# A decoder block in FP32: the first FFN chunk with three interleaved Strassen units and norm weights applied behind the transposes

## The chip, the core and the metric

The kernel runs on one core of one Trainium2 chip. The metric is the device time of one execution in microseconds, and of a set of executions the median. TensorE is written PE, ScalarE ACT, VectorE DVE, GpSimd POOL and SyncE SP.

## What is computed

One layer over 512 tokens of width 1024, all in float32: a retention branch and a block-sparse attention branch, mixed by sigmoid gates, an output product with a residual, and then the SwiGLU FFN with a hidden width of 2816. The change touches the end of the first part and the start of the FFN:

```python
mix = jax.nn.sigmoid(ga) * a + jax.nn.sigmoid(gb) * b
x = x + mix @ w_o[l]
h2 = rmsnorm(x, norm2_w[l])
f = (jax.nn.silu(h2 @ w_ffn_gate[l]) * (h2 @ w_ffn_up[l])) @ w_ffn_down[l]
x = x + f
```

with `rmsnorm(x, w) = x * rsqrt(mean(x*x) + 1e-6) * w`.

## The kernel before

**Number format.** Every operand of a large product is split into a high part in the reduced format fp32r (a cast on ACT, tiles `wh` for weights and `h`, first half, for activations) and a low part, the remainder (a subtraction on DVE, tiles `wl` and `h`, second half). `mm3` issues three matmuls for one product: high x high, high x low, low x high.

**Strassen units.** Most of the large products are done in the Strassen-Winograd form: seven products of quarter matrices instead of eight. The activations are the quarters A11, A12 (upper 256 tokens, first and second half of the features), A21, A22 (lower 256 tokens) and the sums S1 = A21 + A22 up to sign, S2, S3, S4, made by DVE and split like all else. The weights are B11, B21, B22 and the sums T1, T2, T3, T4: T1 and T3 come by a load and an accumulating transfer on POOL's queue, T2 is a sum on DVE, T4 is a sum on DVE or an accumulating transfer into T2's buffer once T2 has been split (`was_split`, L380). A unit (`wino_unit`) covers 128 gate columns twice and 128 up columns twice, two tiles of the hidden width. Each product is 2 x 4 calls of `mm3`, 24 matmuls. Its results are collected in PSUM banks X, Y and Z; Z is one bank for the whole program (`zbank`, in the trace `pm_233`). X is copied out behind B11 (`p1`, into `fa`) and behind T2 (`u2`, into `fb`), because T2 and T3 go on accumulating in it; Y behind T1 (`p5`). Z takes A12 x B21, which `c11` adds to the copy of X.

**The FFN.** `CHUNKS = (6, 6, 6, 4)` tiles of the hidden width, in units of two. The first chunk has three units: the first (`PLAIN`, `plain_unit`) is done without Strassen as eight products, four with the upper tokens and then four with the lower; the second has the order `DOWN`, the third `ENDING`. After each chunk comes its share of the down product. `Hidden` holds what happens to the results of a unit: Silu of the gate half, product with the up half, and the split and sums for the down product.

**Between the two parts.** The output product `w_o` is a unit with `Residual(squares, 0.5)`: its results are added to `xr`, squared on ACT with a sum (`squares`), and when a half of the tokens is complete `norm_rows` makes the row factor and `xn = xr * factor * norm weights` on DVE. `turned` transposes `xn` on PE, four transposes for two feature tiles; `h2_put` splits straight out of PSUM; `keep` in `h2_turn` also copies the whole into `f`, which the sums need. For the upper tokens this happens during the last product of `w_o`, at the places that `TURN` gives. For the lower tokens `h2_lower` does it after the third product of the plain unit (`before_last`), all 16 transposes in a row, and then plans the sums S1 to S4 with `later(n, ...)`, n half-products further.

**Order of the work.** Nothing is scheduled by the tool: each engine does its instructions in the order in which the program writes them. `advance`, called after each half product, counts the ticks of `later` and emits the split of the next weight piece (`piece_emit`) as far as the caps (`PAHEAD`, `FAHEAD`) allow; `porder` is the order of the pieces, `loads` that of the loads. A load is issued on SP when a raw buffer comes free (`used`).

Of the kernel before, what the change touches and what calls it, by code (L numbers as in the profile page):

```python
# [51 lines left out]
WARM = 12  # L52
T4CHUNKS = 52
LANE = 4
TURN = (0, 1, 2, 1)
WQ = 2
RGATE = (2, 0)
SUMS = 2
# [2 lines left out]
OAHEAD = (6, 10)  # L61
SLACK = 1000
MARGIN = 0
HLAG = 1
LLAG = 1
CHUNKS = (6, 6, 6, 4)
# [5 lines left out]
V_N1, V_Q, V_K = 0, 8, 9  # L72
V_ALL = 10

NORMAL = "B11 T1 *1 T2 B21 B22 T3 / T4"
ENDING = "B11 T1 *1 T2 B21 B22 T3 T4w"
PLAIN = "B11 B21 B12 B22"  # L80
DOWN = "B11 B21 T1 T2 B22 T3 / T4"
ALONE = "B11 B21 T1 T2 B22 T3 T4z"


def weight_plan():

    units = []

# [12 lines left out]

    halves = (range(4), range(4, 8))  # L110

    def cols(col):
        units.append(("X", ("w_in", halves, col, 256), NORMAL))

    units += [("M", (C_MQ, 0)), ("M", (C_MQ, 4)), ("M", (C_MK, 0)), ("M", (C_MK, 4))]
    cols(C_MV)
    for name, i in ORDER:
        if name == "rg":
            cols(C_RG + 512 * i)
        elif name == "rv":  # L120
            cols(C_RV + 512 * i)
        elif name == "rk":
            wino("w_in", C_RQ + 256 * i, "w_in", C_RK + 256 * i)
        elif name == "a":
            feat(sum([group("w_ret_out", (4 * i + ct) * P, KT) for ct in range(4)], []))
        elif name == "b":
            feat(sum([group("w_moba_out", (4 * i + ct) * P, 4) for ct in range(4)], []))
        else:
            c = {"ga": C_GA, "gb": C_GB}[name] + 512 * i
            wino("w_in", c + 256, "w_in", c)  # L130
    units.append(("X", ("w_o", halves, 0, 512), ALONE))
    for c in range(len(CHUNKS)):
# [32 lines left out]


@with_exitstack
def hybrid_block(ctx: ExitStack, tc: tile.TileContext, wall, xin, xtok, n2, cin, out):
    nc = tc.nc
    plan = weight_plan()  # L170
    NU = len(plan)
# [89 lines left out]
    def later(n, f):  # L261
        later_q.append([n, f])
# [21 lines left out]
    for u, unit in enumerate(plan):  # L284
        chunk_of[u] = chunk
        if unit[0] in "WX":
# [7 lines left out]
            if unit[2] == PLAIN:  # L294
                loads += [(u, (q, 0), [chunk + c]) for q, c in (("B11", 0), ("B21", 3), ("B12", 1), ("B22", 2))]
                porder += [(u, (q, 0)) for q in order]
                for q in order:
                    width[u, (q, 0)] = 1024
# [30 lines left out]
    def load_w(parts=1, queue=None):  # L329
        if wstate["load"] >= len(loads):  # L330
            return []
        u, q, cs = loads[wstate["load"]]
        wstate["load"] += 1
        t = raw[u, q] = big(nm("raw"))
        uses[u, q] = 2 if isinstance(q, tuple) and plan[u][2] != PLAIN and (q[0] == "B22" or q[0] == "B21" and u not in t4dma) else 1
# [438 lines left out]
    def wino_finish():  # L774
        if wpend:
            wpend.pop(0)()

    def wino_prod(w, u, bank, m, q, start, stop, out, copies=None, hold=False):

        kind, what = plan[u][:2]  # L780
# [2 lines left out]
        for j, n in enumerate(ws):  # L783
            pc = piece(u, (q, j))
            for i in (0, 1):
# [16 lines left out]
                advance(0 if hold and (j, i) != (0, 0) or copies and (j, i) in ((len(ws) - 2, 1), (len(ws) - 1, 0)) else 1)  # L802
# [6 lines left out]
    def wino_unit(w, ev, hooks={}):  # L809

        u = cur[0]
        cur[0] += 1
# [9 lines left out]

        def third(*x):
            ev.c22(*x)
            if "T4w" in order:
                ev.u3(*x)

        def first(*x):
            ev.p1(*([*x, bank("Z")] if seed else x))

        whole = "T4w" in order or "T4z" in order
# [8 lines left out]
        def run(q):  # L840
# [2 lines left out]
                      bank("Z") if q == "T3" and "T4z" in order else None,  # L843
                      q == "T4z")

        rest = False
        for q in order:
            if q == "/":
# [6 lines left out]
            else:  # L855
                run(q)
                if q in hooks:
                    hooks[q]()

    def plain_unit(w, ev, before_last):  # L860

        u = cur[0]
        cur[0] += 1
        for r in (0, 1):
            for n, out in enumerate((ev.gate, ev.up)):
                ps = main_ps()
                for x, q in enumerate((("B11", "B21"), ("B12", "B22"))[n]):
                    if (r, n, x) == (0, 1, 1):
                        before_last()
                    pc = piece(u, (q, 0))  # L870
                    for i in (0, 1):
                        for k in range(4):
                            mm3(ps[:, i * 256:(i + 1) * 256], pc[:, (4 * i + k) * P:(4 * i + k + 1) * P],
                                w(("A11", "A12", "A21", "A22")[2 * r + x], k), i == k == x == 0, x == 1 and k == 3, True)
                        if (r, i) == (1, 1):
                            piece_done(u, (q, 0))
                        advance(1)
                        run_bg(1)
                later(1, lambda r=r, ps=ps, out=out: out(r, ps))

    class Quarters:

# [554 lines left out]
    n2r = big("n2r")  # L1437
    nc.sync.dma_start(n2r, n2)

    class Residual:  # L1440

# [60 lines left out]
    h2 = Wino("h2")  # L1502

# [16 lines left out]

    def h2_turn(r):

        pss = []

        def keep(j):
            if j % 2 == 0:
                f2[r, j], f2[r, j + 1] = halves(nm("f"))
            A.copy(f2[r, j], pss[j])  # L1528

        def step(j):  # L1530
            pss.append(turned(r, j))
            h2_put(("A11", "A12", "A21", "A22")[2 * r + j // 2], j % 2, pss[j])()
            if j:
                keep(j - 1)
            if j == 3:
                keep(3)
                del xn[2 * r], xn[2 * r + 1]

        return [lambda j=j: step(j) for j in range(4)]
# [1 line left out]
    def h2_lower():  # L1541
# [13 lines left out]
        def rest():  # L1555
            lows.pop(0)()
            lows.pop(0)()

        later(1, lambda: sums_of("S1", (1, 2), (1, 0)))
# [4 lines left out]
        later(6, lambda: sums_of("S3", (0, 0), (1, 0)))  # L1564
        later(6, rest)
        later(7, rest)

    wstate["cap"] = OAHEAD
    more_raws(OEXTRA)
# [12 lines left out]
    assert not turn  # L1582


    class Hidden:
# [43 lines left out]
        def gate(self, r, x):  # L1629
            A.activation((self.a0, self.a1)[r], x, AF.Silu)  # L1630

        def up(self, r, x):
            if r:
                self.lower(x)
            else:
                self.upper(x)

        def upper(self, up):

# [53 lines left out]
    for c in range(len(CHUNKS)):  # L1693
# [7 lines left out]
                later_step()  # L1701
            return mats[m, k]

        for k, f in enumerate(chunk_tiles(c)[::2]):
            if f == 0:
                wstate["cap"] = PAHEAD
                plain_unit(h2, Hidden(mats, k), h2_lower)
            else:
                wstate["cap"] = FAHEAD
# [68 lines left out]
```

## Time and profile before

| | us |
|---|---|
| runs, lowest / median / highest of 3 | 782.83 / 783.02 / 783.41 |
| the profiled execution | 781.12 |
| its span | 779.2 |
| PE busy in it | 772.2 |
| DVE busy | 630.3 |
| ACT busy | 457.2 |

The span runs from the first to the last instruction of the profiled execution; its own time has what lies around that as well. Instructions of an engine overlap a little at their ends, so the time from one start to the next is shorter than a row's duration. Nearly all of the code is issued through one helper, so its line L220 says nothing; the operations are told apart by the names of their tiles.

### The profile page before, as it was taken

To read this page: it belongs to the slowest core of one execution; us is meant where nothing else is said; L and a number is where in the kernel's file an instruction comes from. 1 tells how busy PE (TensorE), PEld (TensorE's weight loads), DVE (VectorE), ACT (ScalarE), POOL (GpSimd) and SP (SyncE) were. 2 spreads that over 40 slices of the span, in tenths; PEclk is the share of its full clock that TensorE was granted. 3 is DMA by queue.
4 is the path that set the end of the run, shared out by engine and by line. 5 is a ranking of instruction groups with operands and counts; after the bars stand their busy time and mean duration, and the time that the engine had idled before them with its cause. 6 is when DMAs were issued, how large, how long until landed. Compare 5 with 4: busy or idle time off the path is not lost.

```text
span 779.2 us, 13656 instructions
## 1 busy us (share of the span) xinstructions
PE 772.2 (99%) x5394; PEld 711.6 (91%) x5394; DVE 630.3 (81%) x959; ACT 457.2 (59%) x750; POOL 69.0 (9%) x83
## 2 busy tenths in 40 slices
PE   9999999999999999999999999999999999999997
PEld 6889988899999998989988898988999899988996
DVE  7988778897788687758589798899787987789787
ACT  8655677774695485634356765654554455655442
POOL 0000100010101000000001000111001110110000
PEclk9999999999999999999999999999999999999999
DMA  9854753556677484654999614789556894779502
GB/s 325 284 130 114 162 131 88 136 140 159 188 167 187 124 221 114 166 133 127 256 328 257 167 32 108 180 208 298 163 137 161 258 269 109 170 200 287 128 1 108
DMA packets 40671, 134.86 MB, mean 173 GB/s; under 512 B 4512, under 2 KB 5024, under 8 KB 40608
## 3 DMA queue, kind: packets, MB, share of 16 engines
q1 hardware_dynamic: 28512, 93.75, 34.5%
q0 software_dynamic: 11376, 39.06, 28.7%
q10 hardware_dynamic: 720, 1.18, 0.4%
q8 instruction: 42, 0.69, 0.4%
q14 instruction: 21, 0.17, 0.1%
HBM read 131.88 MB, written 2.10 MB: 172 GB/s over the span
## 4 chain that ended last, share of the span: by engine, by line
PE 87%; DVE 6%; issue 3%; DMA 2%; ACT 1%; POOL 0%; DVEq 0%; ACTq 0%; POOLq 0%
PE pm L220 79%; PE ps L220 8%; DMA raw<-wall 2%; DVE wl L220 1%; DVE h L220 1%; DVE ws L220 1%; DVE xn L220 1%; DVE xr L220 0%; ACT wh L416 0%; ACT f L1528 0%; DVE mx L220 0%; POOL raw L343 0%; ACT h L1516 0%; ACT sq L1485 0%; DVE qb L220 0%
## 5 line engine op out<-in xcount | busy, mean ns | idle before, releaser
L220 DVE TENSOR_TENSOR wl<-raw,wh 128x1024 fp32r<-128x1024 f32 x209 | 252.2, 1220 | 39.5 <-ACT wh L416 32.7
L416 ACT CAST wh<-raw 128x1024 fp32r<-128x1024 f32 (+1 forms) x230 | 225.1, 1008 | 50.5 <-DVE raw L220 28.7
L220 PE MATMUL pm<-h,wh 128*128 128x256 f32 x1248 | 225.4, 283 | 1.6 <-ACT fa L1595 0.8
L220 PEld LDWEIGHTS pm<-h,wh 128*128 128x128 f32 x1248 | 195.0, 192 | 2.5 <-ACT fa L1595 1.0
L220 PE MATMUL pm<-h,wl 128*128 128x256 f32 x624 | 176.6, 283 | 0.0
L220 PEld LDWEIGHTS pm<-h,wl 128*128 128x128 f32 x624 | 119.7, 192 | 0.0
L343 POOL DMA_DIRECT2D raw<-wall x60 | 55.4, 924 | 442.1 <-DMA raw<-wall 244.0
L220 PE MATMUL pm<-hS,wh 128*128 128x256 f32 x384 | 71.0, 285 | 0.0
L220 PE MATMUL pm<-wh,hA 128*128 128x256 f32 (+1 forms) x304 | 68.6, 310 | 0.0
L220 PE MATMUL pm<-wh,hS 128*128 128x256 f32 x320 | 62.5, 286 | 0.0
L220 PEld LDWEIGHTS pm<-hS,wh 128*128 128x128 f32 x384 | 60.0, 192 | 0.6 <-issue 0.3
L220 PE MATMUL pm<-hS,wl 128*128 128x256 f32 x192 | 54.3, 283 | 0.0
L220 PE MATMUL pm<-hA,wh 128*128 128x256 f32 x288 | 53.7, 285 | 0.0
L220 PEld LDWEIGHTS pm<-wh,hA 128*128 128x128 f32 x304 | 50.9, 191 | 2.8 <-ACT p L1060 0.2
L220 PEld LDWEIGHTS pm<-wh,hS 128*128 128x128 f32 x320 | 51.5, 191 | 0.0
L220 DVE TENSOR_TENSOR raw<-raw,raw 128x1024 f32<-128x1024 f32 (+1 forms) x41 | 48.2, 1181 | 0.4
L220 PE MATMUL pm<-wl,hA 128*128 128x256 f32 (+1 forms) x152 | 46.4, 305 | 0.0
L220 PEld LDWEIGHTS pm<-hA,wh 128*128 128x128 f32 x288 | 45.2, 192 | 0.4
L220 PE MATMUL pm<-wl,hS 128*128 128x256 f32 x160 | 45.2, 283 | 0.0
L220 PE MATMUL pm<-hA,wl 128*128 128x256 f32 x144 | 40.7, 283 | 0.0
L220 PE MATMUL pm<-wh,gsh 128*128 128x512 f32 x112 | 39.8, 390 | 0.0
L220 PE MATMUL pm<-ret,wh 128*128 128x512 f32 x128 | 39.5, 390 | 0.0
(250 smaller groups left out, 1393.4 us busy)
## 6 DMA issues: line engine op xcount, KB each, us to landing
raw<-wall SPq DMA_DIRECT2D x155, 512.0 KB, 4.8
raw<-wall POOLq DMA_DIRECT2D x70, 512.0 KB, 7.0
raw<-wall SPq DMA_DIRECT2D x19, 256.0 KB, 3.5
raw<-wall POOLq DMA_DIRECT2D x9, 256.0 KB, 7.3
xr<-xtok SPq DMA_DIRECT2D x4, 512.0 KB, 7.2
x<-xin SPq DMA_DIRECT2D x7, 256.0 KB, 5.0
out<-xr SPq DMA_DIRECT2D x7, 256.0 KB, 2.1
raw<-wall ACTq DMA_DIRECT2D x4, 256.0 KB, 6.2
```

The lines of the kernel that those rows point to most:

```text
L220: return f(out, *args, **kw)
L343: nc.gpsimd.dma_start(t[:, s], wall[c, :, s], accum_op=ALU.add)
L416: A.copy(h, src)
```

## The change

1. All three units of the first chunk become Strassen units (`FIRST`), and their products are interleaved by a table, `SCRIPT`. The number ahead of a product is that of the unit. The six products B11 and B21 of the three units come first; they need upper tokens only. Then unit 0's T1, T2, B22, T3, and the rest. `plain_unit` goes; `wino_unit` is cut in two, and `wino_start` gives a function that runs one product.
2. T4 of all three comes by an accumulating transfer (`t4dma`). The last one has a bank of its own (T4w).
3. `h2_lower` is called after the third product as before, which now is unit 1's B11 (`LOWER`).
4. The norm weights are no longer in `xn`. The upper `xn` is a `tensor_scalar` on DVE, the lower one an ACTIVATE with a scale on ACT. Behind the transposes the features lie on the partitions, and two ACTIVATEs of 256 columns with the norm weight as scale (`vec[:, V_N2 + ...]`) make `f` out of PSUM; `h2_put` splits from `f`. A21 is not split any more, since no Strassen product reads it; A22 is split at the end (`last`). The transfer of the norm weights in row form (`n2r`) goes.
5. `TURN` has five places for the upper transposes instead of four: two of the four sets now stand in the middle of unit 0's first product.
6. In that first product one tick of `advance` emits no weight piece.

```diff
-TURN = (0, 1, 2, 1)
+TURN = (0, 1, 1, 0, 2)
+LOWER = "1 B11"
-PLAIN = "B11 B21 B12 B22"
+FIRST = "B11 B21 T1 T2 B22 T3 T4"
+SCRIPT = ("0 B11", "0 B21", "1 B11", "1 B21", "2 B11", "2 B21", "0 T1", "0 T2", "0 B22", "0 T3", "1 T1", "0 T4",
+          "1 T2", "1 B22", "1 T3", "2 T1", "1 T4", "2 T2", "2 B22", "2 T3", "2 T4w")
...
-            order = ENDING if f == fs[-2] else NORMAL
-            if f < 4:
-                order = (PLAIN, DOWN)[f // 2]
+            order = FIRST if c == 0 else ENDING if f == fs[-2] else NORMAL
...
+            if unit[2] == FIRST:
+                t4dma.add(u)
+                if plan[u - 1][2] != FIRST:
+                    table = dict(WLOAD)
+                    for x in SCRIPT:
+                        v, q = int(x[0]), x[2:5].rstrip("w")
+                        porder.append((u + v, (q, 0)))
+                        if q in table:
+                            loads.append((u + v, (q, 0), [chunk + 4 * v + c for c in table[q]]))
...
-                V.scalar_tensor_tensor(xn[2 * r + i][:, c], xr[2 * r + i][:, c], y[:, i:i + 1], n2r[:, c],
-                                       ALU.mult, ALU.mult)
+                o, x, f = xn[2 * r + i][:, c], xr[2 * r + i][:, c], y[:, i:i + 1]
+                if r:
+                    A.activation(o, x, AF.Copy, scale=f)
+                else:
+                    V.tensor_scalar(o, x, f, None, ALU.mult)
...
-            A.copy(f2[r, j], pss[j])
-
-        def step(j):
-            pss.append(turned(r, j))
-            h2_put(("A11", "A12", "A21", "A22")[2 * r + j // 2], j % 2, pss[j])()
+            f = f2[r, j]
+            for k in (0, 1):
+                c = slice(k * 256, (k + 1) * 256)
+                A.activation(f[:, c], ps[:, c], AF.Copy, scale=vec[:, V_N2 + 2 * j + k:V_N2 + 2 * j + k + 1])
+            if r == 0:
+                h2_put(("A11", "A12")[j // 2], j % 2, f)()
...
+        if c == 0:
+            wstate["cap"] = PAHEAD
+            runs = [wino_start(h2, Hidden(mats, k))[0] for k in range(CHUNKS[0] // 2)]
+            for x in SCRIPT:
+                runs[int(x[0])](x[2:])
+                if x == LOWER:
+                    h2_lower()
+                if x == "0 T1":
+                    wstate["cap"] = FAHEAD
```

Three places show how the engines' queues change. The first is ACT at the transposes of the upper tokens, behind the weight casts. Tiles `ps` are the transposed sets, `h` the split quarters A11 and A12, `sq` the squares of the lower tokens. Before:

```order
L1516 CAST h_638_5109<-ps_5104 128x512
L1485 ACTIVATE sq_5118,ss_4780<-xr_4772 128x512
L1516 CAST h_641_5125<-ps_5120 128x512
L1528 COPY f_5128<-ps_5104 128x512
L1516 CAST h_644_5135<-ps_5130 128x512
L1528 COPY f_5128<-ps_5120 128x512
```

Now:

```order
L1528 ACTIVATE f_5108<-ps_5103,vec 128x256 x2
L1512 CAST h_639_5111<-f_5108 128x512
L1478 ACTIVATE sq_5120,ss_4778<-xr_4772 128x512
L1528 ACTIVATE f_5108<-ps_5122,vec 128x256 x2
L1512 CAST h_642_5129<-f_5108 128x512
```

The cast of the first set no longer reads PSUM; it follows two scalings (the row with x2) and reads their result, and the second set follows a square as before.

The second is ACT from the row factor of the lower tokens (`r_s`) to their transposes; `wh` are weight casts, `ps` the transposed sets of the lower tokens. Before:

```order
L509 ACTIVATE r_s<-n2v 128x2
L416 CAST wh_5213<-raw_4914 128x1024
L1630 ACT_TABLE_LOAD
L1630 ACTIVATE fa_5159<-pm_5161 128x512
L1516 CAST h_662_5272<-ps_5267 128x512
L1516 CAST h_664_5280<-ps_5275 128x512
L1528 COPY f_5283<-ps_5267 128x512
L1516 CAST h_667_5290<-ps_5285 128x512
```

Now:

```order
L1494 ACTIVATE xn_5210<-xr_4772,r_y 128x512
L1494 ACTIVATE xn_5211<-xr_4773,r_y 128x512
L1596 COPY fa_5141<-pm_5147 128x512
L423 CAST wh_5229<-raw_4888 128x1024
L423 CAST wh_5245<-raw_4912 128x1024
L1608 ACT_TABLE_LOAD
L1608 ACTIVATE fa_5141<-fa_5141 128x512
L423 CAST wh_5264<-raw_4932 128x1024
L1528 ACTIVATE f_5286<-ps_5281,vec 128x256 x2
L1528 ACTIVATE f_5286<-ps_5289,vec 128x256 x2
L1528 ACTIVATE f_5301<-ps_5296,vec 128x256 x2
L1528 ACTIVATE f_5301<-ps_5304,vec 128x256 x2
```

The four `xn` have come to this queue from DVE, a third weight cast and the `fa` of unit 0's gate half stand ahead of the transposes' readers, and each reader is a pair of scalings.

The third is DVE from the first sum of S1 to the add out of the Z bank (`fa` from `pm_233`). Before, that add stood behind the whole of the plain unit; the rows from S1's sums on are:

```order
L220 TENSOR_TENSOR ws_5317<-f_5302,f_5283 128x512
L220 TENSOR_TENSOR ws_5321<-f_5302,f_5283 128x512
L220 SCALAR_TENSOR_TENSOR ws_5337<-ws_5317,f_5128 128x512
L220 SCALAR_TENSOR_TENSOR ws_5341<-ws_5321,f_5128 128x512
L220 TENSOR_TENSOR h_672_5319<-ws_5317,h_672_5319 128x512
L220 TENSOR_TENSOR h_674_5323<-ws_5321,h_674_5323 128x512
L220 TENSOR_TENSOR fb_5160<-pm_5241,fa_5159 128x512
L220 TENSOR_TENSOR h_676_5339<-ws_5337,h_676_5339 128x512
```

Now:

```order
L223 TENSOR_TENSOR ws_5324<-f_5301,f_5286 128x512
L223 TENSOR_TENSOR ws_5328<-f_5301,f_5286 128x512
L223 SCALAR_TENSOR_TENSOR ws_5348<-ws_5324,f_5108 128x512
L223 SCALAR_TENSOR_TENSOR ws_5352<-ws_5328,f_5108 128x512
L223 TENSOR_TENSOR h_674_5326<-ws_5324,h_674_5326 128x512
L223 TENSOR_TENSOR h_676_5330<-ws_5328,h_676_5330 128x512
L223 TENSOR_TENSOR wl_5358<-raw_4932,wh_5332 128x1024
L223 TENSOR_TENSOR wl_5361<-raw_4953,wh_5334 128x1024
L223 TENSOR_TENSOR fa_5143<-pm_233,fa_5143 128x512
```

The last row is the add of unit 1. The sums S1 and S2, S1's low parts and the low parts of two weight pieces stand directly ahead of it.

## Rows read from the trace of the kernel before

**Rows 1.** The page, part 1: the span, and TensorE's busy time, share and matmuls.

```profile
span 779.2 us, 13656 instructions
...
PE 772.2 (99%) x5394; PEld 711.6 (91%) x5394; DVE 630.3 (81%) x959; ACT 457.2 (59%) x750; POOL 69.0 (9%) x83
```

**Rows 2.** TensorE's waits for other engines: total us, times, longest.

```profile
PE pm L220 <- ACT fa L1595: 0.8, 1, 0.8
PE pm L220 <- ACT fa L1598: 0.8, 1, 0.8
```

**Rows 3.** Two stretches: busy us (instructions) by engine, granted clock, DMA share, GB/s.

```profile
445.00:450.00 5.00, 5.00 (x44) 5.00 (x43) 3.18 (x11) 4.34 (x7) 0.00 (x0) 1.00 0.00 0
475.00:480.00 5.00, 3.49 (x27) 3.29 (x28) 3.37 (x6) 3.13 (x6) 0.00 (x0) 1.00 0.62 194
```

**Rows 4.** TensorE in order of time: start, us, operation, count.

```profile
436.78 0.60 PE L220 MATMUL ps<-cst,xn 128*128 128x128 f32 x4
...
441.23 0.48 PE L220 MATMUL pm<-h,wh 128*128 128x256 f32 x2
...
443.11 0.40 PE L220 MATMUL pm<-h,wh 128*128 128x256 f32 x2
...
443.47 0.40 PE L220 MATMUL pm<-h,wh 128*128 128x256 f32 x2
...
449.95 1.91 PE L220 MATMUL ps<-cst,xn 128*128 128x128 f32 x16
```

**Rows 5.** ScalarE and TensorE at the two waits, in order of time.

```profile
475.09 0.58 ACT L1595 COPY fa<-pm 128x512 f32<-128x512 f32 x1
...
475.72 0.51 PE L220 MATMUL pm<-h,wh 128*128 128x256 f32 x2 [0.84 <-ACT fa L1595]
...
479.65 0.50 PE L220 MATMUL pm<-h,wh 128*128 128x256 f32 x2 [0.79 <-ACT fa L1598]
```

**Rows 6.** ScalarE in order of time around the transposes.

```profile
434.74 2.00 ACT L416 CAST wh<-raw 128x1024 fp32r<-128x1024 f32 x2
437.42 0.59 ACT L1516 CAST h<-ps 128x512 fp32r<-128x512 f32 x1 [0.68 <-PE ps L220]
437.90 0.63 ACT L1485 ACTIVATE sq<-xr 128x512 f32<-128x512 f32 x1
...
447.90 1.28 ACT L1630 ACT_TABLE_LOAD   x1
449.20 0.60 ACT L1630 ACTIVATE fa<-pm 128x512 f32<-128x512 f32 x1
```

**Rows 7.** Groups by form and a ScalarE pair: busy us, mean ns; then start, us.

```profile
L1011 ACT ACTIVATE qa<-pm,r_y 128x256 f32<-128x256 f32 x4 | 1.7, 472 | 2.5 <-PE pm L220 2.5
...
L220 DVE TENSOR_SCALAR hf<-x,xv 128x512 f32<-128x512 f32 x7 | 3.4, 481 | 0.0
...
65.78 0.84 ACT L1011 ACTIVATE qa<-pm,r_y 128x256 f32<-128x256 f32 x2 [1.41 <-PE pm L220]
```

**Rows 8.** VectorE in order of time around the transposes.

```profile
431.66 0.15 DVE L220 TENSOR_TENSOR n2v<-ss 128x2 f32<-128x2 f32 x1
...
433.28 2.74 DVE L220 SCALAR_TENSOR_TENSOR xn<-xr,r_y,n2r 128x512 f32<-128x512 f32 x4
...
437.14 2.35 DVE L220 TENSOR_TENSOR wl<-raw,wh 128x1024 fp32r<-128x1024 f32 x2
...
458.87 1.29 DVE L220 TENSOR_TENSOR h<-ws,h 128x512 fp32r<-128x512 f32 x2
```

**Rows 9.** The page, part 6: accumulating transfers, count, KB, us to landing.

```profile
raw<-wall POOLq DMA_DIRECT2D x70, 512.0 KB, 7.0
```

**Rows 10.** TensorE's first work, and two stretches at the end of the span.

```profile
1.19 5.23 PE L540 MATMUL ps<-warmb 128*128 128x512 bf16 x12 [1.19 <-DVE warm L220]
...
775.00:776.00 1.00, 0.10 (x1) 0.00 (x0) 0.75 (x2) 0.00 (x0) 0.00 (x0) 1.00 0.92 342
778.00:779.20 1.20, 0.00 (x0) 0.00 (x0) 0.00 (x0) 0.00 (x0) 0.00 (x0) 0.50 0.00 0
```

More of the change, by code (lines that the diff above doesn't have):

```diff
@@ L63 @@
 MARGIN = 0
+PHOLD = 3
+LOWER = "1 B11"
 HLAG = 1
@@ L70 @@
 K_ALL = 1568
-V_N1, V_Q, V_K = 0, 8, 9
-V_ALL = 10
+V_N1, V_Q, V_K, V_N2 = 0, 8, 9, 10
+V_ALL = 18
 NORMAL = "B11 T1 *1 T2 B21 B22 T3 / T4"
 ENDING = "B11 T1 *1 T2 B21 B22 T3 T4w"
-PLAIN = "B11 B21 B12 B22"
 DOWN = "B11 B21 T1 T2 B22 T3 / T4"
 ALONE = "B11 B21 T1 T2 B22 T3 T4z"
+FIRST = "B11 B21 T1 T2 B22 T3 T4"
+SCRIPT = ("0 B11", "0 B21", "1 B11", "1 B21", "2 B11", "2 B21", "0 T1", "0 T2", "0 B22", "0 T3", "1 T1", "0 T4",
+          "1 T2", "1 B22", "1 T3", "2 T1", "1 T4", "2 T2", "2 B22", "2 T3", "2 T4w")
 def weight_plan():
@@ L167, in hybrid_block @@
 @with_exitstack
-def hybrid_block(ctx: ExitStack, tc: tile.TileContext, wall, xin, xtok, n2, cin, out):
+def hybrid_block(ctx: ExitStack, tc: tile.TileContext, wall, xin, xtok, cin, out):
     nc = tc.nc
@@ L293, in hybrid_block @@
                     width[u, (q, j)] = n
[L294 to L298, printed above, removed]
+            if unit[2] == FIRST:
[7 more added lines that the diff above has]
+                            loads.append((u + v, (q, 0), [chunk + 4 * v + c for c in table[q]]))
                 chunk += 4
@@ L334, in load_w @@
         t = raw[u, q] = big(nm("raw"))
-        uses[u, q] = 2 if isinstance(q, tuple) and plan[u][2] != PLAIN and (q[0] == "B22" or q[0] == "B21" and u not in t4dma) else 1
+        uses[u, q] = 2 if isinstance(q, tuple) and (q[0] == "B22" or q[0] == "B21" and u not in t4dma) else 1
         w = width[u, q]
@@ L776, in wino_finish @@
             wpend.pop(0)()
+    firsts = [u for u, x in enumerate(plan) if x[0] == "W" and x[2] == FIRST]
     def wino_prod(w, u, bank, m, q, start, stop, out, copies=None, hold=False):
@@ L801, in wino_prod @@
                     A.copy(copies[i], bank[i])
-                advance(0 if hold and (j, i) != (0, 0) or copies and (j, i) in ((len(ws) - 2, 1), (len(ws) - 1, 0)) else 1)
+                advance(0 if hold and (j, i) != (0, 0) or u == firsts[0] and m == "A11" and q == "B11" or copies and (j, i) in ((len(ws) - 2, 1), (len(ws) - 1, 0)) else 1)
                 if j == len(ws) - 1 and half == 512:
@@ L807, in wino_prod, with wino_start @@
                 run_bg(1)
-    def wino_unit(w, ev, hooks={}):
+    def wino_start(w, ev):
         u = cur[0]
@@ L824, in third @@
             ev.c22(*x)
-            if "T4w" in order:
+            if own:
                 ev.u3(*x)
@@ L829, in first @@
             ev.p1(*([*x, bank("Z")] if seed else x))
-        whole = "T4w" in order or "T4z" in order
+        own = "T4w" in order or u == firsts[-1]
+        whole = own or "T4z" in order
         seed = not wide and order[1] != "B21"
@@ L844, in run, with wino_unit @@
                       q == "T4z")
+        return run, order
+    def wino_unit(w, ev, hooks={}):
+        run, order = wino_start(w, ev)
         rest = False
@@ L858, in wino_unit @@
                     hooks[q]()
[L860 to L879, printed above, removed]
     class Quarters:
@@ L1436, in hybrid_block @@
         nc.sync.dma_start(xr[t], xtok[:, t, :])
-    n2r = big("n2r")
-    nc.sync.dma_start(n2r, n2)
     class Residual:
@@ L1521, in h2_turn, with step @@
     def h2_turn(r):
-        pss = []
-        def keep(j):
+        def step(j):
+            ps = turned(r, j)
             if j % 2 == 0:
                 f2[r, j], f2[r, j + 1] = halves(nm("f"))
-            A.copy(f2[r, j], pss[j])
-        def step(j):
-            pss.append(turned(r, j))
-            h2_put(("A11", "A12", "A21", "A22")[2 * r + j // 2], j % 2, pss[j])()
-            if j:
-                keep(j - 1)
+            f = f2[r, j]
[4 more added lines that the diff above has]
+                h2_put(("A11", "A12")[j // 2], j % 2, f)()
             if j == 3:
-                keep(3)
                 del xn[2 * r], xn[2 * r + 1]
@@ L1557, in rest, with last @@
             lows.pop(0)()
+        def last():
+            for j in (0, 1):
+                lows.append(h2_put("A22", j, f2[1, 2 + j]))
         later(1, lambda: sums_of("S1", (1, 2), (1, 0)))
@@ L1563, in h2_lower @@
         later(5, lambda: sums_of("S4", "S2", 2))
-        later(6, lambda: sums_of("S3", (0, 0), (1, 0)))
         later(6, rest)
-        later(7, rest)
+        later(7, lambda: sums_of("S3", (0, 0), (1, 0)))
+        later(8, rest)
+        later(9, last)
+        later(10, rest)
     wstate["cap"] = OAHEAD
@@ L1581, in hybrid_block @@
     wino_unit(mx, Residual(squares, 0.5), {"T3": lambda: bg.extend([lambda n=n: turn_steps(n) for n in TURN])})
-    assert not turn
+    assert len(turn) == TURN[-1]
     class Hidden:
@@ L1627, in c21 @@
             later(1, lambda: self.lower(self.b1))
[L1629 to L1636, printed above, removed]
         def upper(self, up):
@@ L1702, in hidden @@
             return mats[m, k]
[L1704 to L1709, printed above, removed]
+        if c == 0:
[7 more added lines that the diff above has]
+                    wstate["cap"] = FAHEAD
+        else:
+            for k in range(CHUNKS[c] // 2):
                 wino_unit(h2, Hidden(mats, k))
@@ L1765 @@
     xin[:, V_K] = np.tile(np.asarray(inputs["k_norm_w"])[0], 2)
+    xin[:, V_N2:V_N2 + 8] = np.asarray(inputs["norm2_w"])[0].reshape(KT, P).T
     xtok = np.ascontiguousarray(x.reshape(NT, P, D).transpose(1, 0, 2))
-    n2 = np.ascontiguousarray(np.broadcast_to(np.asarray(inputs["norm2_w"])[0], (P, D)))
-    arrays = {"wall": wall, "xin": xin, "xtok": xtok, "n2": n2, "cin": _consts()}
+    arrays = {"wall": wall, "xin": xin, "xtok": xtok, "cin": _consts()}
     nc = bacc.Bacc("TRN2", target_bir_lowering=False, num_devices=1)
```

## The prediction

> **What bounds the kernel now.** I read the page first, then PE's waits, then PE, ScalarE (ACT) and VectorE (DVE) in order of time around the change. PE is busy 772.2 of the 779.2 us span [rows 1]; between its first and last matmul it waits only twice for another engine that the trace names, 0.8 us each [rows 2]. So time is saved by giving PE fewer matmuls or by taking those two waits away, and every new wait of PE is paid in full. Both lie in the first FFN chunk, the stretch that is rewritten: in its worst 5 us PE is busy 3.49 [rows 3]. The profiled execution took 781.12 us, 1.9 more than its span; the median of the runs is 783.02, another 1.9. I sum against the span and add the same 3.8 for the median.
>
> **What goes.** A Strassen unit has seven products where the plain unit had eight. A product is 24 matmuls of 256 columns; three of them start 0.36 us ahead of the next three [rows 4], so 24 x 0.12 = **2.88 us** go. The 32 transposes keep their count. The two old waits have one form: a copy out of a bank that PE needs back stands on ACT behind weight casts and work on the lower half; the first copy runs from 475.09 for 0.58, and PE goes on at 475.72; the waits are 0.84 and 0.79 [rows 5]. In the new order six products stand between that copy's source (0 B11) and the bank's next use (0 T2), so it is covered; the other (T1's bank, used by B22) comes back, below. I take off both, **1.63**, and count the second again where it stands.
>
> **What comes, on the path.** For each wait I follow the new order of ACT and DVE with durations of before, on the clock of before.
>
> (a) The first two products. Before, a 512-wide cast read the transposes directly, 0.59 us [rows 6]. Now two half-width ACTIVATEs with a scale per row come first, then the cast, out of their result. The nearest row is the same shape from PSUM with a per-row scale, 0.84 for two, of which one takes some 0.47, so 0.37 from one to the next [rows 7]. The transposes start at 436.78 [rows 4], ACT starts at 437.42 [rows 6]: 0.84 + 0.59 to 438.9; a square and the read of its sum 0.7; the second pair and cast to 441.1; DVE's low part 0.69: 441.8. PE, with only two sets of transposes ahead of 0 B11, starts that product at 440.4 and asks for this part 0.84 later: **0.5** of wait. The A12 half: two sets of transposes in the middle of 0 B11, from 442.4; pair, cast, pair, cast on ACT, 2.9 from 443.1 to 446.0; the low parts on DVE end at 445.3 and 446.7. PE is through with 0 B11 at 444.6 and asks for the first at 444.75, for the second 0.7 after that: **0.5** and **0.6**. Together **1.6**; between 0.3 (scaling as cheap as the old copies, 0.48 apart for 512 columns) and 2.6 (no overlap of the half-width ACTIVATEs).
>
> (b) Unit 1's B21 writes the Z bank, one bank for all three units, and must wait until DVE has added unit 0's product out of it. That add (fa from pm_233) stands on DVE behind the low part of a weight piece, whose cast stands on ACT behind the four xn of the lower half, which moved there. The last lower square, behind those casts, ends at 446.6; the row factor takes 1.6 [rows 8]; a 512-wide scaling on ACT lies between a copy, 0.48 from one to the next [rows 6], and two half-widths, 0.74 [rows 7]: I take 0.6, the middle, so 450.6; copy 0.5, cast 0.95, low part 1.2, add 0.7: 453.9. PE, through with 1 B11 at 451.4 and with 16 transposes (1.67 us [rows 4]) at 453.1, waits **0.8**; 0 to 1.5.
>
> (c) Unit 2's B21 waits for unit 1's add out of the same bank, and the rest of PE's queue behind it. This is the large one. On ACT there follow a second cast (to 453.0), the table load, 1.28 [rows 6], the Silu that waits for (b)'s add (to 454.7), a third cast (455.6), and only then the eight half-width scalings of the lower half, whose transposes are ready by 453.1: 8 x 0.37, to 458.7. On DVE two sums of S1 (the first from 458.1), two of S2 and S1's two low parts at 0.6 each [rows 8], then two weight low parts at 1.13 stand ahead of the add: 458.1 + 3.7 + 2.3 = 464.1, and the add 0.7: 464.8. PE is done with 1 B21 at 456.8 and with 2 B11 at 459.7. **5.1** of wait, 4.0 to 6.0. ACT's rows show a Silu 1.30 after the load's start [rows 6], so the load costs its own 1.28. The Trainium skill (ScalarE: Activation LUTs, What ACT_TABLE_LOAD costs) gives about 2.66 us for a switch, the load and a drain. By that (c) would be some 1.4 longer; I go by the row.
>
> (d) 0 B22 needs T1's bank copied out (fa from pm). DVE, late since (c), does two weight low parts (2.3) and eight 512-wide operations at 0.6 (S2's low parts, S4's sums and low parts, S3's sums) from 464.8: 471.9; then unit 2's add out of Z, 472.5, for which a Silu on ACT waits; behind it the two casts of A22 (1.0) and the copy: 474.7. PE, going again at 464.8, has 2 B21, 0 T1 and 0 T2 (8.64) to do: 473.4. **1.3**, 0.3 to 2.
>
> (e) Unit 2's T3 needs the copy behind its T2 (fb from pm). Ahead of it on ACT is the cast of unit 2's T4, whose weights come by an accumulating POOL transfer that is issued only after its T2 has been split. Such transfers take 7.0 us at the median [rows 9]; behind the cast come a Silu, another weight cast and three casts of unit 1's products, 3.5 at their own durations, before the copy. PE comes to T3 two products, 5.8, after T2's start, and T2's weights are split some products ahead. **1.0**, 0 to 2.5; I can't place it better than that from rows of before.
>
> **What is hidden.** Three more weight pieces are split (seven where four were used twice): 3 x 1.05 on ACT and 3 x 1.2 on DVE, in part counted above, otherwise beside PE. DVE gives four xn (2.74 together) to ACT, does the other four in about 0.48 each [rows 7, 8] and has two fewer low parts, so its total hardly moves; its order is what costs. SP loses the 512 KB of norm weights and gains one load; POOL gains four accumulating transfers. The DMA engines move nothing from 445 to 450 [rows 3], so bandwidth covers them; if it did not, (e) is where it would show.
>
> **Sum.** -2.88 - 1.63 + 1.6 + 0.8 + 5.1 + 1.3 + 1.0 = +5.3.
>
> (f) The clock. PE's last 0.10 us of work lies in 775 to 776, still at a granted clock of 1.00, the 2.4 GHz level; from 778 it stands at 0.50, the 1.2 GHz level. The warm-up, PE's first work, shows 12 matmuls of 512 columns in 5.23 us, 0.44 each, the lower level's pace [rows 10]. Wait (c) leaves PE idle longer than the end did before the clock stood at half, so PE may restart at 1.2 GHz. If that lasted as long as the warm-up, some 25 matmuls would take 0.1 more each: 2.5, of which (d), a wait for other engines, gives 1.3 back. Between 0 and +1.2; I take +0.5. Total **+5.8**: span 785.0, profiled execution 786.9, median 788.8. About 0.2% (1.6 us) can be told from no change.
>
> **Rivals.** *The gain arrives* (faster). The place is unit 2's B21: if the Z bank is free by 459.7, (c) is nothing, (d) and (e) go with it, and -2.88 - 1.63 with 1.6 of small waits gives -2.9: 780.1. Against it: the add is the ninth operation on DVE behind the lower half's scalings, and ACT and DVE together must take 5 us less than their rows say. For it: half-width ACTIVATEs may overlap more than I count, and 2 B11 runs beside them. It decides at waits summing to under 3 us. Chance 0.12. *A wash:* waits of 3 to 6 in all, (c) at 4 and nearly all others at their lower ends: 783 +- 1.6. Chance 0.08. *The slow clock is paid too*, for as long as in the warm-up, and (e) stands at its upper end: 5.3 + 1.2 + 1.5 = +8.0, 791.0. For it: the idle stretch is long; against it: PE is dense on both sides of it. Chance 0.18. The Trainium skill (TensorE: Matmul & The Clock Gate, Part 1) has the throttled state as the default, which activity releases. By that rule a long wait is paid a second time after it ends; the tail's rows agree, and no row of before shows a restart within the kernel.
>
> **How the numbers follow.** Forecast (waits of 6.5 to 11.5 in all, +2 to +7) 0.62. Slower by over 0.2%: 0.62 + 0.18 = 0.80; within: 0.08; faster: 0.12. The range leaves out the gain and the wash, 0.20, and takes in the rest: from 785.0 (+2) to 792.0, a little beyond the slow clock's time.
>
> **What would show it.** Right: 24 fewer matmuls; among PE's waits one of 4 to 6 us for DVE's add out of the Z bank near 460, small ones for h and fa between 441 and 454, one for an ACT copy near 474; a granted clock under 1.00 just behind the large one if (f) is paid. Wrong: no PE wait over 2 us between 455 and 466, or waits for weights late in the chunk that are larger than all of these, which would mean that the transfers, not the bank, have become the limit.

## The result and the profile after

The changed kernel takes 788.25 us (median of 4 runs, 788.06 to 788.68), the kernel before beside it 782.92 (782.19 to 783.41): ratio 1.0072, 95% interval 1.0057 to 1.0087. It is slower by 5.3 us. The profiled execution took 788.24 us, its span is 786.5.

From the page, its first part; the 24 matmuls are gone [rows 1], yet PE's busy time has grown by 1.1 us:

```profile
span 786.5 us, 13627 instructions
## 1 busy us (share of the span) xinstructions
PE 773.3 (98%) x5370; PEld 711.2 (90%) x5370; DVE 631.5 (80%) x960; ACT 465.1 (59%) x766; POOL 72.5 (9%) x87
```

PE's waits between 436 and 520 us (engine, line, what it waited for: us in total, times, longest); they stand in place of the two of [rows 2]:

```profile
PE pm L223 <- DVE fa L223: 5.5, 2, 5.0
PE pm L223 <- DVE h L223: 0.9, 3, 0.3
PE pm L223 <- ACT fb L1602: 0.9, 1, 0.9
```

Where they stand, in PE's timeline (start, us, engine, line, operation, tiles; in brackets the idle time ahead and who ended it):

```profile
442.00 0.38 PE L223 MATMUL pm<-h,wh 128*128 128x256 f32 x1 [0.27 <-DVE h L223]
442.22 0.28 PE L223 MATMUL pm<-h,wl 128*128 128x256 f32 x1
...
445.61 0.39 PE L223 MATMUL pm<-h,wh 128*128 128x256 f32 x1 [0.32 <-DVE h L223]
...
447.00 0.39 PE L223 MATMUL pm<-h,wh 128*128 128x256 f32 x1 [0.34 <-DVE h L223]
...
454.39 0.51 PE L223 MATMUL pm<-h,wh 128*128 128x256 f32 x2 [0.46 <-DVE fa L223]
...
465.46 0.77 PE L223 MATMUL pm<-h,wh 128*128 128x256 f32 x2 [5.05 <-DVE fa L223]
...
470.59 0.40 PE L223 MATMUL pm<-h,wh 128*128 128x256 f32 x2
...
507.90 0.28 PE L223 MATMUL pm<-h,wl 128*128 128x256 f32 x1
509.08 0.51 PE L223 MATMUL pm<-h,wh 128*128 128x256 f32 x2 [0.90 <-ACT fb L1602]
...
514.94 0.40 PE L223 MATMUL pm<-wh,gu 128*128 128x512 f32 x1
```

The first three waits are (a) of the prediction, then come (b), (c) and (e). The row at 470.59 is the first matmul of the product behind 2 B21. The last row is the first matmul of the down projection, the end of the rewritten stretch. In PE's timeline of the kernel before it is this one, 6.40 us earlier:

```profile
508.54 0.40 PE L220 MATMUL pm<-wh,gu 128*128 128x512 f32 x1
```

The stretch by windows of 5 us (length, PE busy and its matmuls, granted clock, DMA share, GB/s):

```profile
455.00:460.00 5.00, 5.00 (x44) 1.00 0.01 3
460.00:465.00 5.00, 0.41 (x4) 0.86 0.00 0
465.00:470.00 5.00, 4.54 (x21) 0.50 0.90 160
470.00:475.00 5.00, 5.00 (x42) 0.96 0.55 102
```

PE stood still from 460.4 to 465.5. The granted clock fell to 0.50, the 1.2 GHz level, within the gap, and stayed there while PE worked again: 21 matmuls start in 4.54 busy us, where 455 to 460 has 44 in 5.00. It was back at 1.00, 2.4 GHz, by 471. ScalarE and VectorE before the long wait, each in order of time:

```profile
448.50 2.56 ACT L1494 ACTIVATE xn<-xr,r_y 128x512 f32<-128x512 f32 x4 [1.02 <-DVE r_y L223]
...
451.43 2.00 ACT L423 CAST wh<-raw 128x1024 fp32r<-128x1024 f32 x2
453.45 1.28 ACT L1608 ACT_TABLE_LOAD   x1
454.74 0.63 ACT L1608 ACTIVATE fa<-fa 128x512 f32<-128x512 f32 x1
...
456.22 3.02 ACT L1528 ACTIVATE f<-ps,vec 128x256 f32<-128x256 f32 x8
...
474.60 0.59 ACT L1599 ACTIVATE fa<-pm 128x512 f32<-128x512 f32 x1
```

```profile
452.51 1.23 DVE L223 TENSOR_TENSOR wl<-raw,wh 128x1024 fp32r<-128x1024 f32 x1 [4.05 <-ACT wh L423]
...
458.75 1.28 DVE L223 TENSOR_TENSOR ws<-f,f 128x512 f32<-128x512 f32 x2
459.95 1.29 DVE L223 SCALAR_TENSOR_TENSOR ws<-ws,f 128x512 f32<-128x512 f32 x2
461.15 1.29 DVE L223 TENSOR_TENSOR h<-ws,h 128x512 fp32r<-128x512 f32 x2
462.36 2.35 DVE L223 TENSOR_TENSOR wl<-raw,wh 128x1024 fp32r<-128x1024 f32 x2
464.63 0.68 DVE L223 TENSOR_TENSOR fa<-pm,fa 128x512 f32<-128x512 f32 x1
```

The last row is the add that frees the Z bank for 2 B21. Its product was ready at about 457; it runs ninth behind the lower half's scalings on ScalarE, as the prediction had counted. And some 6 us ahead of this train VectorE had been idle for 4.05 us, until 452.51, behind a weight cast that on ScalarE stood behind the four row pieces (xn).

### The profile page after: what moved, and what is told of

Read it like the earlier page. It is cut to its first block, busy times and chain, and to the rows that moved or that the text cites. A ratio compares the mean times of both kernels' runs of the same rounds, so it can differ in the third digit from the quotient of the medians.

```text
span 786.5 us, 13627 instructions
## 1 busy us (share of the span) xinstructions
PE 773.3 (98%) x5370; PEld 711.2 (90%) x5370; DVE 631.5 (80%) x960; ACT 465.1 (59%) x766; POOL 72.5 (9%) x87
## 3 DMA queue, kind: packets, MB, share of 16 engines
q10 hardware_dynamic: 720, 1.18, 0.4%
## 4 chain that ended last, share of the span: by engine, by line
PE 78%; issue 6%; DVE 5%; DMA 5%; ACT 5%; POOL 1%; DVEq 0%; SPq 0%; POOLq 0%; ACTq 0%
PE pm L223 70%; PE ps L223 7%; DMA raw<-wall 5%; DVE wl L223 2%; ACT wh L423 1%; PE ps L547 1%; DVE ws L223 0%; POOL raw L350 0%; ACT f L1528 0%; DVE fb L223 0%; DVE rot L223 0%; DVE h L223 0%; ACT xn L1494 0%; DVE xr L223 0%; ACT rot L1175 0%
## 5 line engine op out<-in xcount | busy, mean ns | idle before, releaser
L223 DVE TENSOR_TENSOR wl<-raw,wh 128x1024 fp32r<-128x1024 f32 x212 | 256.1, 1220 | 48.7 <-ACT wh L423 42.0
L423 ACT CAST wh<-raw 128x1024 fp32r<-128x1024 f32 (+1 forms) x233 | 228.6, 1008 | 59.4 <-DVE raw L223 34.6
L350 POOL DMA_DIRECT2D raw<-wall x62 | 57.5, 933 | 430.7 <-DMA raw<-wall 226.4
L387 POOL DMA_DIRECT2D raw<-wall x21 | 18.1, 863 | 233.8 <-DVE wl L223 203.0
```

Of the source, the lines that this page charges most:

```text
L223: return f(out, *args, **kw)
L387: nc.gpsimd.dma_start(t[:, w], wall[chunk_of[u] + 3 * n + q[1], :, w], accum_op=ALU.add)
L423: A.copy(h, src)
```

## The experiments

The theory after the result: ScalarE's and VectorE's queues deliver the lower half's data too late, and PE pays wherever it first needs something from them, with the slow clock on top. The rival is the prediction's own wording, that the shared Z bank is the cause. Medians in us, each with the kernel before on the same chip:

| run | this | before | ratio (95%) |
|---|---|---|---|
| the change | 788.25 | 782.92 | 1.0072 (1.0057 to 1.0087) |
| e1_filler | 787.25 | 782.65 | 1.0060 (1.0045 to 1.0075) |
| e2_own_bank | 789.47 | 782.65 | 1.0088 (1.0073 to 1.0103) |
| e3_xn_dve | 784.78 | 782.65 | 1.0030 (1.0019 to 1.0041) |
| e4_t4_sum | 787.45 | 782.65 | 1.0060 (1.0043 to 1.0076) |
| e5_norm_only | 783.49 | 782.51 | 1.0013 (1.0004 to 1.0023) |
| e6_old_norm | 785.72 | 782.51 | 1.0040 (1.0027 to 1.0054) |
| e7_best | 780.93 | 782.51 | 0.9978 (0.9969 to 0.9987) |
| e8_best_old_norm | 781.28 | 782.51 | 0.9983 (0.9974 to 0.9992) |
| e9_swap | 785.46 | 782.70 | 1.0038 (1.0025 to 1.0050) |
| e10_best_no_swap | 782.30 | 782.70 | 1.0001 (0.9992 to 1.0010) |

**What the slow clock costs (e1).**

```diff
             for x in SCRIPT:
+                if x == "2 B21":
+                    fill = side_ps()
+                    for _ in range(FILL):
+                        nc.tensor.matmul(fill, lhsT=warmb[:, :P], rhs=warmb, start=True, stop=True)
                 runs[int(x[0])](x[2:])
```

> Edit: 18 matmuls on zeros, of which nothing is read, stand in TensorE's queue right ahead of 2 B21, so that TensorE works through most of the 5.05 us gap; nothing else is touched. Theory (the granted clock of 0.50 after the gap is a cost of its own, about 2.5 us for the 5.1 us that TensorE worked at it): the clock stays at 1.00 from 460 to 475, and the time falls by 2.5 less what the products after 2 B21 then wait for lower-half data that they now reach sooner (0 to 1.5 us): 786.5, between 785.5 and 787.3. Rival 1 (those products would wait for VectorE in any case, the slow clock costs nothing): 788.2 +- 0.4. Rival 2 (the added matmuls do not hold the clock): 788.2, with 0.50 still granted after 465.

PE's timeline and windows of this run:

```profile
460.42 4.06 PE L1704 MATMUL ps<-warmb 128*128 128x512 bf16 x18
465.53 0.50 PE L224 MATMUL pm<-h,wh 128*128 128x256 f32 x2 [1.05 <-DVE fa L224]
...
468.50 0.40 PE L224 MATMUL pm<-h,wh 128*128 128x256 f32 x2
...
475.40 0.50 PE L224 MATMUL pm<-h,wh 128*128 128x256 f32 x2 [0.98 <-ACT fa L1600]
```

```profile
465.00:470.00 5.00, 4.47 (x37) 1.00 0.85 158
470.00:475.00 5.00, 4.42 (x37) 1.00 0.56 107
```

2 B21 starts at the same place, now at the full clock, and the kernel is 4.6 us slower than before in place of 5.3. In the trace the way from 2 B21's first matmul to the end of the work ahead of wait (e) takes 42.72 us in the changed kernel (465.46 to 508.18) and 41.78 here (465.53 to 507.31). That is 0.94 less, although a wait of 0.98 has appeared: 0 B22 for the copy of T1's bank, the prediction's (d). The slow stretch itself is read from 2 B21's 24 matmuls: 5.13 us from the first to the start of the next product in the changed kernel (465.46 to 470.59), 2.97 here (465.53 to 468.50). So it costs 2.2 us, and a good half of it would have been waited anyway: 0.98 of idle time, 1.24 from start to start (how this is counted stands under *The sum, term by term*).

**Is it the bank? (e2)**

```diff
-                z = zbank if b == "Z" else main_ps()
+                z = zbank if b == "Z" and u not in [firsts[n] for n in (2,)] else main_ps()
```

> Edit: 2 B21 writes a bank of its own instead of the one that all B21 products share; everything else stands in the same order. Theory of the prediction taken at its word (the shared bank is the cause of the 5.05 us): 2 B21 starts at about 460.5, the wait and the half clock go, 780.5 to 782. Rival (the bank is only where the lateness of the lower half's data becomes visible; VectorE is filled without a pause from 456 to 475): the wait moves to the next products that read sums, about 1 us at 0 T1 for S1 and about 5 us at 0 T2 for S2, with the half clock behind it: 788 to 790.

PE's timeline, then one row each of VectorE's and ScalarE's:

```profile
466.10 0.39 PE L223 MATMUL pm<-h,wh 128*128 128x256 f32 x1 [0.80 <-DVE h L223]
...
474.24 0.80 PE L223 MATMUL pm<-h,wh 128*128 128x256 f32 x2 [5.12 <-ACT fa L1599]
```

```profile
463.63 0.68 DVE L223 TENSOR_TENSOR fa<-pm,fa 128x512 f32<-128x512 f32 x1
```

```profile
473.60 0.59 ACT L1599 ACTIVATE fa<-pm 128x512 f32<-128x512 f32 x1
```

2 B21 no longer waits, and the kernel is 1.5 us slower still. This execution runs 1.0 us ahead of the changed kernel's from the first product on (441.01 against 442.00 for the same wait). Take that off, and the add out of Z and the copy of T1's bank stand where they stood: 463.63 against 464.63, 473.60 against 474.60. The two queues do not know of the new bank; PE has only moved its wait to 0 T2 (for S2's low part, 0.80) and to 0 B22 (for T1's copy, 5.12), one product later each than I had written, with the slow clock behind it. The bank was the place, not the cause.

**What makes the queues late (e3).**

```diff
-                if r:
-                    A.activation(o, x, AF.Copy, scale=f)
-                else:
-                    V.tensor_scalar(o, x, f, None, ALU.mult)
+                V.tensor_scalar(o, x, f, None, ALU.mult)
```

> Edit: the four normalised row pieces of the lower half are made by VectorE (4 x 0.48 us) and not by ScalarE (2.56 us). Theory (ScalarE's queue between 448 and 459 is what makes VectorE late: VectorE sat idle for 4.05 us until 452.5 for a weight cast that stood behind these four): casts and scalings start about 2.5 us earlier, the wait at 2 B21 falls from 5.05 to about 3, the clock stays up or nearly, a wait of about 1 appears at 0 T2: 784.5, between 783.3 and 786.5. Rival (VectorE's own work is the bound, it gets 1.9 us more): 788 to 790.

VectorE's and PE's timelines:

```profile
448.26 1.68 DVE L223 TENSOR_SCALAR xn<-xr,r_y 128x512 f32<-128x512 f32 x4
...
461.59 0.68 DVE L223 TENSOR_TENSOR fa<-pm,fa 128x512 f32<-128x512 f32 x1
```

```profile
462.42 0.48 PE L223 MATMUL pm<-h,wh 128*128 128x256 f32 x2 [2.98 <-DVE fa L223]
```

VectorE makes the four row pieces in 1.68 us, in time in which it sat idle; the train's add moves up by 3.04 (464.63 to 461.59), of which 0.24 is this execution's own lead (441.76 against 442.00 at the first wait), so by 2.8; the time falls by 3.2, from 5.3 over the kernel before to 2.1. Of the change's cost, three fifths is this one placement. The clock fell here too, behind a gap of 2.98 us; the wait I expected at 0 T2 is not in this run.

**The small wait late in the chunk (e4).**

```diff
-                t4dma.add(u)
+                if plan[u + 1][2] == FIRST:
+                    t4dma.add(u)
```

> Edit: unit 2's T4 weights are summed by VectorE (1.22 us) as they were before, not by POOL's accumulating transfer. Theory (the 0.90 us wait at unit 2's T3 comes from a weight cast on ScalarE that stands ahead of the copy and waits for POOL's transfer): that wait goes, 787.3, between 786.9 and 787.6. Rival (something else is late there): 788.2 +- 0.3, with a wait at the same product; or a new one of up to 1.2 us where VectorE's added sum stands.

The wait for fb is gone; 0.32 us for VectorE's fb at 499.88 is new, and the kernel stands 4.8 over before, 0.5 less than the change. The cast behind POOL's transfer was the cause of that wait; part of the gain goes back. What it is worth in time these runs don't show: two of the four executions, with a mean granted clock of 0.994, took 787.65 and 788.35, the other two, at 0.998, 786.97 and 787.25, while the change's four stood at 0.994 to 0.996.

**Each half of the change alone (e5, e6).** The norm's half put on the kernel before, of which this is the core:

```diff
-                V.scalar_tensor_tensor(xn[2 * r + i][:, c], xr[2 * r + i][:, c], y[:, i:i + 1], n2r[:, c],
-                                       ALU.mult, ALU.mult)
+                o, x, f = xn[2 * r + i][:, c], xr[2 * r + i][:, c], y[:, i:i + 1]
+                if r:
+                    A.activation(o, x, AF.Copy, scale=f)
+                else:
+                    V.tensor_scalar(o, x, f, None, ALU.mult)
...
-            A.copy(f2[r, j], pss[j])
...
+                A.activation(f[:, c], ps[:, c], AF.Copy, scale=vec[:, V_N2 + 2 * j + k:V_N2 + 2 * j + k + 1])
```

> Edit: the kernel before with one half of the change alone: norm2's weights are multiplied behind the transposes (eight half-width scalings on ScalarE per token half), the lower half's four row pieces are made by ScalarE; the plain first unit and the order of the products stay. Theory (this half of the change costs time by itself, since ScalarE gets 2.56 us of row pieces and 0.27 us more for each 512 columns read from the transposes, just where it feeds VectorE): slower than before by 1.5 to 3, 784.2 to 785.7. Rival (the cost of the whole change comes from the new order alone): 782.7 +- 0.5.

PE's timeline:

```profile
456.56 0.38 PE L220 MATMUL pm<-h,wh 128*128 128x256 f32 x1 [1.07 <-ACT h L1517]
458.30 0.39 PE L220 MATMUL pm<-h,wh 128*128 128x256 f32 x1 [1.35 <-DVE h L220]
```

It costs 1.0 us, less than I expected: PE waits 2.4 for the lower half, and of the two old waits one (0.84) is gone. The other half alone, on the changed kernel:

```diff
-                if r:
-                    A.activation(o, x, AF.Copy, scale=f)
-                else:
-                    V.tensor_scalar(o, x, f, None, ALU.mult)
+                V.scalar_tensor_tensor(o, x, f, n2r[:, c], ALU.mult, ALU.mult)
...
-                A.activation(f[:, c], ps[:, c], AF.Copy, scale=vec[:, V_N2 + 2 * j + k:V_N2 + 2 * j + k + 1])
+            A.copy(f, ps)
```

> Edit: the changed kernel with the other half alone: three Strassen units in the new order, but norm2's weights again multiplied into the normalised rows by VectorE before the transposes (8 x 0.68) and the transposes read by one 512-wide copy. Theory (the two halves' costs add, and ScalarE's part makes the wait at 2 B21 longer by some 2): wait at 2 B21 of 3 to 4 in place of 5.05, time 785.5, between 784.5 and 786.5. Rival (the norm's place does not matter to the new order, VectorE gets 5.4 us of work back): 788 +- 0.5 or more.

```profile
463.38 0.47 PE L223 MATMUL pm<-h,wh 128*128 128x256 f32 x2 [4.08 <-DVE fa L223]
```

PE's timeline has the wait at 2 B21 at 4.08, and the kernel is 3.2 over before. So the new order alone loses, in spite of its 24 matmuls fewer: 3.2; the norm alone 1.0; both 5.3. Together they cost 1.1 more than the two apart. That is not a clean sum: both runs split the upper quarters from the copy `f` and not out of PSUM, and e6 keeps the change's places for the transposes (`TURN`). In e6's trace the clock fell as well, to 0.78 from 465 to 470.

**Exchanging two products (e9).**

```diff
-SCRIPT = ("0 B11", "0 B21", "1 B11", "1 B21", "2 B11", "2 B21", "0 T1", "0 T2", "0 B22", "0 T3", "1 T1", "0 T4",
-          "1 T2", "1 B22", "1 T3", "2 T1", "1 T4", "2 T2", "2 B22", "2 T3", "2 T4w")
+SCRIPT = ('0 B11', '0 B21', '1 B11', '1 B21', '2 B11', '0 T1', '2 B21', '0 T2', '0 B22', '0 T3', '1 T1', '0 T4', '1 T2', '1 B22', '1 T3', '2 T1', '1 T4', '2 T2', '2 B22', '2 T3', '2 T4w')
```

> Edit: the changed kernel with two neighbours in the order exchanged, 0 T1 ahead of 2 B21; nothing else. Theory (ScalarE and VectorE deliver the lower half's data at a pace that one order of the products can't change, so the 5.05 us of idle time is spread over several products; but without one long gap the clock stays at 1.00, and the 1.9 us of the slow stretch are not paid): waits of 3.5 to 5 in all between 455 and 478, none of over 3, 786, between 785 and 787. Rival 1 (the exchange alone takes the wait away, as the bank has a product more to come free): 782 to 783. Rival 2 (the waits move and the clock falls all the same): 788 +- 0.5.

PE's timeline, and a window:

```profile
461.45 0.39 PE L222 MATMUL pm<-h,wh 128*128 128x256 f32 x1 [1.16 <-DVE h L222]
...
464.92 0.50 PE L222 MATMUL pm<-h,wh 128*128 128x256 f32 x2 [0.47 <-DVE fa L222]
...
473.15 0.50 PE L222 MATMUL pm<-h,wh 128*128 128x256 f32 x2 [2.22 <-ACT fa L1598]
```

```profile
470.00:475.00 5.00, 2.78 (x23) 1.00 0.76 193
```

The wait of 5.05 has become three, 3.85 in all, the clock stays at 1.00 in this execution, and the kernel is 2.8 over before in place of 5.3. Of these 2.6 us 0.8 is wait, from start to start (5.2 against 4.4); the rest I put down to the clock, whose slow stretch e1 priced at 2.2. The idle time was not taken away by the order, it was cut up. Nor did that always spare the clock: two of the six executions, at 786.1 and 786.6, have a mean granted clock of 0.997, the other four, at 785.1 to 785.7, one of 0.999 or 1.000.

**A version that beats both (e7, e8, e10).** The pieces together; e8 is the same with the norm's weights ahead of the transposes, e10 without the exchange:

```diff
-PAHEAD = (6, 8)
+PAHEAD = (5, 6)
-TURN = (0, 1, 1, 0, 2)
+TURN = (0, 1, 1, 1, 1)
...
-            A.activation(self.a0, z, AF.Silu)
+            if cur[0] == firsts[0] + 3 and self.k < 1:
+                later(4, lambda: A.activation(self.a0, z, AF.Silu))
+            else:
+                A.activation(self.a0, z, AF.Silu)
```

(and the edits of e3, e4 and e9)

> Edit: the changed kernel with what the runs so far point to, together: the row pieces of both halves on VectorE; unit 2's T4 summed by VectorE; 0 T1 ahead of 2 B21, so that a product of 2.9 us stands between the two that share the bank; unit 0's first Silu (with its table load) four ticks later, behind the lower half's scalings; five weight pieces ahead in place of six; the transposes of the upper half one at a time. Theory (the cost is where ScalarE and VectorE stand in their queues, not the work itself, so most of the 4.5 us that the change takes away can be had): no wait over 2 us, clock 1.00 throughout, 781, between 780 and 782.5, faster than before (782.7). Rival (VectorE is simply full from 450 to 475, what is moved comes back at another product): 783.5 to 786.

> Edit: as the one before it, but with norm2's weights multiplied before the transposes as they were before the change. Theory: the norm's place is worth little once ScalarE does not make the row pieces, 781 +- 1, within 0.7 of the run with the weights behind the transposes. Rival (VectorE is full, so 8 x 0.2 us more on it show in full, or the half-width scalings on ScalarE are what still costs): over 1 us apart from it, on one side or the other.

> Edit: the best version with the products in the order of the change (2 B21 ahead of 0 T1). Theory (the row pieces, T4's sum, the Silu and the pieces ahead bring most, the exchange about 1.7 as it fills the wait at the bank with a product that is ready): 782.6, between 781.6 and 783.6, with waits of 1 to 2.5 at 2 B21 and at a later product. Rival (the exchange brings nothing once VectorE is early): 780.9 +- 0.5.

PE's longest waits between 425 and 540 in e7, and two windows of it:

```profile
PE pm L222 <- ACT fb L1599: 0.8, 1, 0.8
PE pm L222 <- ACT fa L1596: 0.6, 1, 0.6
```

```profile
465.00:470.00 5.00, 4.36 (x37) 1.00 0.74 218
470.00:475.00 5.00, 4.24 (x36) 1.00 0.31 106
```

e7 takes 780.93 us, 1.6 less than the kernel before (ratio 0.9978, 0.9969 to 0.9987), with no wait over 0.8 and the clock at 1.00. So the Strassen form of the first chunk can be had with a gain, once the queues are arranged for it (whether the same arrangements would have helped the kernel before was not tried, nor what the later Silu, `PAHEAD` and `TURN` bring each by itself); with 780.4 to 781.9 in both, e8 shows that where the norm's weights are multiplied is then worth at most a few tenths. Without the exchange (e10) nothing is left of the gain: 782.30, as before. In e10's profiled execution the clock fell behind a wait of 1.86 at 470.52:

```profile
470.00:475.00 5.00, 4.48 (x25) 0.66 0.40 139
```

In others it did not: the four of its ten with a mean granted clock of 0.998 took 783.4 to 784.3, the six at 1.000 781.9 to 782.3, some 1.8 apart. By PE's rows the slow stretch cost that execution 1.5: its 48 matmuls from 470.52 on took 7.34 us, the 48 behind e1's wait at 465.53, at the full clock, 5.85.

## Why the prediction was right

**The sum, term by term.** Gone: 24 matmuls and both old waits, as written. Added, forecast against the idle time in PE's rows: (a) 1.6, 0.93; (b) 0.8, 0.46; (c) 5.1, 5.05; (d) 1.3, nothing; (e) 1.0, 0.90; (f) 0.5, a slow stretch of 2.2.

The rows' idle time is less than what a wait costs. A matmul's next one normally starts 0.12 behind it, and idle time is counted only from its end after 0.28 (507.90 to 509.08 is 1.18, with 0.90 shown as idle): 0.16 more. The second matmul behind a wait starts 0.22 after the first and not 0.12 (442.00 to 442.22): another 0.10. The prediction worked from start to start, without the second part. So counted, (a) is 1.4, (b) 0.6, (c) 5.2 and (e) 1.1, all close to what was forecast; ScalarE's pairs and casts in (a) took what I had given them (0.84 and 0.62 in the rows of after). The two old waits, which I took off at their idle time of 1.63, were worth 2.15.

(d) and (f) belong together. In the trace of the change there is no (d): the slow stretch delays PE by 2.2 us and covers it. Where the clock holds (e1), (d) comes back at 0.98 of idle time, 1.2 in all, inside its range, and the time that the slow clock adds to that is 0.94. This is what the prediction meant by (f), 2.5 less the 1.3 of (d), and it lies within 0 to 1.2, near the upper end; 0.5 was too little. Their sum was forecast at 1.8 and is 2.2. So the rival with the slow clock was close on the clock; (e), which it put at its upper end of 2.5, was not there. The Trainium skill (TensorE: Matmul & The Clock Gate, Part 1) has the throttled state as the default that activity releases. The windows agree, with 0.50 granted from within the gap on and for 5 us of work behind it.

(c) came out by the working in the prediction: three weight casts, a table load, a Silu and eight scalings on ScalarE, then eight operations on VectorE ahead of the add, whose start was forecast for 464.1 and is at 464.63. Of this 0.3 is the later start of the whole stretch (transposes at 437.08, not 436.78 [rows 4]). The working also left out a sum of two weight pieces (1.22 from 457.60 on) that VectorE does directly ahead of S1's sums. The Silu starts 1.29 us behind the start of the table load's 1.28, as before [rows 6]. The 2.66 us that the Trainium skill (ScalarE: Activation LUTs, What ACT_TABLE_LOAD costs) gives for a switch is not what these rows show, and by it (c) would have been 6.5.

**What the sum left out.** It forecast +5.8 between two executions; the spans differ by 7.3. From the first transposes to the down projection (436.78 to 508.54 before, 437.08 to 514.94 after) the difference is 6.1. The idle times and the slow stretch give -2.88 - 1.63 + 0.93 + 0.46 + 5.05 + 0.90 + 2.2 = 5.0; four more waits at 0.26 each make it 6.1. So this stretch is accounted for, and 0.3 above the forecast. A further 0.8 stands in the down projection itself, where PE now waits once for a weight's low part (0.19 shown, at 527.78; about half of the 0.8 is not in this wait, and open), and 0.3 ahead of the transposes. Neither place was in the sum.

That the median came out at 788.25, so close to 788.8, is in part luck. I took the profiled execution to stand 1.9 under the median, as the one before did; the one after stands at its median. The forecast for the profiled execution, 786.9, was 1.3 too low, and this base 1.9 too large. What made that execution of before quick was not tried; no other execution of that kernel here was under 782.17.

**What was wrong in the reasoning.** The rival "the gain arrives" was said to decide at one place, the Z bank free by 459.7, with (d) and (e) going along. e2 frees it and is slower. (d), which that rival let go, grew there from 1.3 to 5.1. The other half of that sentence was right: ScalarE and VectorE have to be some 5 us earlier. e3 gets 2.8 of them by filling VectorE's idle time, which the prediction's rows did not show because it lies in the kernel after. Of DVE the prediction said that "its total hardly moves; its order is what costs": the total was no measure here, since VectorE stood idle for 4.05 us while ScalarE did the four xn that had been taken from it.

## What to carry to other kernels

A wait names the last thing that came; before the bank, the buffer or the semaphore it names is given more room, ask when the next thing that PE needs from the same queue will be ready: if that is as late, the wait moves. An operation is given to another engine by who is idle ahead of the train that matters, not by totals. And one long gap can cost more than the same idle time in pieces, by the clock behind it (here in most executions, not in all): place a product that is ready between two that share a bank.

## What the runs showed of the hardware

The granted clock fell inside the kernel behind a gap, and the matmuls after it went at half pace for 5 us: 2.2 us for a gap of 5.05. It also fell behind gaps of 4.08 (e6), 2.98 (e3), 1.86 (e10) and, in the trace of e8, 1.72 (0.73 granted from 470 to 475). Waits of 1.16, 0.47 and 2.22 us spread over 12 us (e9) left it at 1.00. So the length of the gap alone does not decide it. Nor is it the same in every execution of one kernel: six of e10's ten have a mean granted clock of 1.000, and two of e9's six one of 0.997; their gaps were not traced. Eighteen matmuls on zeros, 4.06 us, held it at 1.00 through the gap.
